# A hybrid decoder layer: VectorE, ScalarE and SyncE put into program order, with loads further ahead

## The chip, the cores and the metric

The kernel runs on one core of a Trainium2 chip. The metric is the device time of one execution in microseconds (us). TensorE (PE) does the matrix products, VectorE (DVE) and ScalarE (ACT) the elementwise work, GpSimd (POOL) a few powers, and SyncE (SP) issues nearly all DMAs. Each of these engines takes its instructions from one queue.

## The reference

One decoder layer over 256 tokens of 2048 features, in float32:

```python
hn = rmsnorm(h, norm_mix_w[l])
q, k, v, g_ret, xr, yr, g_a, g_b = jnp.split(hn @ w_in[l], offsets, axis=-1)
...
ret = head_groupnorm(chunkwise_retention(q, k, v), ret_gn_w[l]).reshape(b, s, D_RET_V)
ret_out = jax.nn.silu(g_ret) * ret
xr = causal_dwconv(xr, rnn_conv_w[l], rnn_conv_b[l])
hr = rg_lru(xr, rg_w_a[l], rg_b_a[l], rg_w_x[l], rg_b_x[l], rg_lambda[l])
rnn_out = jax.nn.gelu(yr) * hr
merged = (jax.nn.sigmoid(g_a) * (ret_out @ w_proj_ret[l])
          + jax.nn.sigmoid(g_b) * (rnn_out @ w_proj_rnn[l]))
h = h + merged @ w_mix_out[l]
...
h = h + memory_cross_attention(hn, mem_n, xa_w_q[l], xa_w_k[l], xa_w_v[l], xa_w_o[l])
...
h = h + conv_gated_ffn(hn, ffn_w_up[l], ffn_conv_w[l], ffn_conv_b[l], ffn_w_down[l])
return rmsnorm(h, final_norm_w)
```

Retention has 8 heads with rotary positions; the RG-LRU is a gated recurrence over the tokens (here four blocks of 512 features); the cross-attention has 4 heads over 256 memory tokens; the FFN is 5632 wide, with a convolution over three tokens ahead of its gate.

## The kernel before

All weights lie in one stream in the order of use (`weight_plan`). A chunk of it is four tiles of 128 rows by 512 columns, 1 MB, loaded by SP into one of three `raw` buffers. `prefetch` splits each chunk into a rounded part `hi` (ACT, two instructions) and the rest `lo` (DVE, two instructions), in six buffers each, which is three chunks; the products x_hi·w_hi + x_lo·w_hi + x_hi·w_lo on TensorE stand for a float32 product. One chunk is 24 matmuls of 512 columns, or as much in other shapes. Before the matmuls of chunk c are written down, the chunks up to c+2 are split (`AHEAD`), so the split of c+3 is written behind everything that follows chunk c. It needs the `hi` and `lo` buffers of chunk c.

Four chunks make a product of 256 tokens by 512 columns. Its result is read out of PSUM (`turned_rows`: DVE writes `rows`), cut by ACT into 16-bit planes (`by_dma`: `pl`, two copies), transposed by two DMAs (`pt`), and joined by ACT (`f`, two copies). The call `later(n, fn)` has a function run n + 1 chunks further on; the joins, the attention scores and the recurrence are written in this way between the chunks.

The parts that the change and the prediction touch, in the order of the layer:

- `tables` and `rotated`: sine and cosine, and the rotation of q and k (ta, tb, an add, and a split into s by ACT and DVE).
- `retain`: scores, values, and `normalise`, which scales the rows of each head (rc, on DVE) and writes them (ACT), two tiles of two pairs of heads each.
- `conv_x`, `recur`, `gelu_y`, once for each of the four blocks of the RG-LRU: the convolution over four tokens (one ACT and three DVE instructions for each of four tiles, `xr`); the gates with small products on TensorE, tanh and exp on ACT, a square root, and a scan on DVE; and the gelu of the other branch, the product `rn`, and its split into s. `RG_WAIT` sets how many chunks the recurrence comes behind the convolution.
- `gated`: the sigmoid gates of the merge; `residual`: adding to the residual rows, their squares and their transposes; `memory_steps`: the norm of the memory; `gate_up`: the gated product of the FFN and its split.

What sets the order: matmuls and the small transposes on TensorE are kept in the order of the program (`mm`, `turn_small`). All else is ordered by the tile scheduler, which places each instruction by its priority and by when it expects the operands; `high_priority` moves the evacuation and the planes ahead. So on ACT, DVE and SP a split may stand ahead of work that was written before it.

Of the kernel before, what the change touches and what calls it, by code (L numbers as in the profile page):

```python
# [36 lines left out]
FREE = 300  # L37
RG_WAIT = 3
EPS = 1e-6
# [88 lines left out]


@with_exitstack  # L130
def hybrid_layer(
# [72 lines left out]

    def mm(*a, **k):
        tc.keep_in_program_order(pe.matmul(*a, **k))  # L206

    def turn_small(*a):
        tc.keep_in_program_order(pe.transpose(*a))  # L209

# [15 lines left out]
    at = [0]  # L226

    def prefetch(n):
        while len(ahead) < n and taken[0] < len(stream):
            i = taken[0]  # L230
            name, row, nk, c = stream[i]
            taken[0] += 1
            size = nk * P * BW
            src = wall[at[0] : at[0] + size].rearrange("(p k n) -> p k n", p=P, k=nk)
            at[0] += size
            raw = wp.tile([P, KC, BW], F32, tag="raw", bufs=RAW_BUFS, name=nm("raw"))
            k2 = row // (KH * P)
# [3 lines left out]
            if own:  # L241
                xs.load(k2 + 1)
            for a, b in zip(cuts, cuts[1:]):
                sp.dma_start(out=raw[:, a:b, :], in_=src[:, a:b, :])  # L244
                if i == 0 and a == 0:
                    sp.dma_start(out=xs.rest[0], in_=xs.rest[1])
                elif own and a == 0:
                    xs.load(k2 + nk // KH)
# [10 lines left out]
            for k in range(0, nk, KH):  # L259
# [13 lines left out]
                parts.append((hi, lo))  # L273
            ahead.append(((row, c), parts))
            if i >= 4:
                load_x(min(4, i - 3))
# [30 lines left out]
    def steps_t(w, row, st, nk, col):  # L307
# [4 lines left out]
        for k0, n, parts in chunks(nk, w, row, col):  # L312
            last = k0 + n >= nk
            tiles = [(kk, j) for j in range(2) for kk in range(n)]
            if first and k0 == 0:
                runs = [[(t, pr, kk, j) for t in (0, 1)] for kk in range(n) for pr in range(2) for j in range(2)]
            elif last:
                runs = [[(t, pr, kk, j) for kk, j in tiles] for pr in range(2) for t in (1 - pr, pr)]
            else:
                runs = [[(t, pr, kk, j) for pr in range(2) for kk, j in tiles] for t in (phase, 1 - phase)]  # L320
                phase = 1 - phase
            for i, run in enumerate(runs):
                for t, pr, kk, j in run:
                    k = k0 + kk
                    sx = st[k // 2][:, k % 2, :]
                    part = parts[kk // KH][t][:, kk % KH, (2 * pr + j) * P : (2 * pr + j + 1) * P]
                    a = accs[pr][:, j, :]
                    if t == 1:
                        a, sx = a[:, S:BW], sx[:, 0:S]
                    mm(  # L330
                        a, part, sx, start=k == 0 and t == 0, stop=k == nk - 1 and t == 0, skip_group_check=True
                    )
# [7 lines left out]
    def products_n(o, sx, hi, lo, tt, start, stop):  # L340
        h = sx[:, tt * P : (tt + 1) * P]
        l = sx[:, S + tt * P : S + (tt + 1) * P]
        mm(o, h, hi, start=start, stop=False)
        mm(o, l, hi, start=False, stop=False)
        mm(o, h, lo, start=False, stop=stop)

# [16 lines left out]
    def product(o, l, r, start, stop):  # L363

        for i, (a, b) in enumerate(((l[0], r[0]), (l[0], r[1]), (l[1], r[0]))):
            mm(o, a, b, start=start and i == 0, stop=stop and i == 2, skip_group_check=True)

# [101 lines left out]
    def spread_tokens(r):  # L469
# [5 lines left out]
        def products():  # L475
            bc = small((P, S))
            for tt in range(2):
                cs = slice(tt * P, (tt + 1) * P)
                mm(bc[:, cs], ones, diag[:, cs], start=True, stop=True)
            act.copy(rsb, bc)  # L480
# [97 lines left out]
    qjoin = [joined(t, "q") for t in next(q_steps)]  # L578
    assert next(q_steps, None) is None
    later(0, tables)  # L580

# [21 lines left out]
    def retain(g, qr, kr, vs, dec, gates):  # L603
# [36 lines left out]
        def normalise():  # L640
            rows = [big([P, 2, BW], s="rows") for _ in range(2)]
            rstd = rsqrt_small(stats[:, :, 1], 8, 1.0, GN_EPS).rearrange("p (h t) -> p h t", t=2)
            for tt in range(2):
                dve.tensor_scalar_mul(rstd[:, :, tt], rstd[:, :, tt], rs0[:, tt : tt + 1])
            for hh in range(4):
                for tt in range(2):
# [5 lines left out]
                    )  # L652
                    act.mul(rows[hh // 2][:, tt, (hh % 2) * DV : (hh % 2 + 1) * DV], y, rstd[:, hh, tt : tt + 1])  # L653
            for i, r in enumerate(rows):
                by_dma(r, words.append, 2 + i)

# [64 lines left out]
    def recur(b, rgw, xr, pr, aa, tt_, ti):  # L721

        for j in (2 * pr, 2 * pr + 1):
# [3 lines left out]
            for i in range(2):  # L727
                mm(gp[:, i, :], rgw[:, i, j, :], xr[:, j, :], start=True, stop=True)
            tr = tp.tile([P, S], F32, tag="tr", bufs=2, name=nm("tr"))
# [17 lines left out]
        for j in range(4):  # L747
            dve.tensor_tensor_scan(
                out=xr[:, j, :], data0=aa[:, j, :], data1=ti[:, j, :], initial=0.0, op0=ALU.mult, op1=ALU.add
            )  # L750

    for b in range(4):
# [27 lines left out]
        def gelu_y(f, xr=xr):  # L780
            for pr in range(2):
                y = f[:, 2 * pr : 2 * pr + 2, :]
                y2, th = tmp("y2"), tmp("yt")
                act.activation(y2, y, AF.Square)
                dve.tensor_scalar(out=y2, in0=y2, scalar1=0.044715 * K0, scalar2=K0, op0=ALU.mult, op1=ALU.add)
                dve.tensor_tensor(out=y2, in0=y2, in1=y, op=ALU.mult)
                act.activation(th, y2, AF.Tanh)
                dve.scalar_tensor_tensor(out=y, in0=th, scalar=1.0, in1=y, op0=ALU.add, op1=ALU.mult)
            for pr in range(2):
                o = tmp("rn")  # L790
                cs = slice(2 * pr, 2 * pr + 2)
                dve.tensor_tensor(out=o, in0=xr[0][:, cs, :], in1=f[:, cs, :], op=ALU.mult)
                rnn.append(split_pair(o, 0.5))

        turned_rows(gemm_n("w_in", 0, xs, NT, O_XR + b * BW), rs0, conv_x)
        turned_rows(gemm_n("w_in", 0, xs, NT, O_YR + b * BW), rs0, gelu_y, 4 if b < 3 else 3)


# [29 lines left out]
    def residual(w, st, out, wcol, steps=None):  # L828

        ss = sums()  # L830
        for b in range(4):
            if steps:
                steps(b)
            h = hrow[b]
            dve.tensor_add(h, h, gemm_n(w, 0, st, NT, b * BW))  # L835
            squares(h, ss, b)
            by_dma(hrow[b], lambda f, b=b: turn(f, b, out, wcol))
        return ss
# [15 lines left out]
    def memory_steps(b):  # L854
        if b == 1:
            ss = sums()
            for c in range(4):
                sum_squares(mnat[c], ss, c)
            rsms.append(rstd_rows(ss))
        if b == 3:  # L860
# [35 lines left out]
    def transpose_probs(pr_):  # L896
        t = small()
        for kt in range(2):
            for tt in range(2):
                turn_small(t[:, kt, tt * P : (tt + 1) * P], pr_[:, tt, kt * P : (kt + 1) * P], ident)  # L900
        if done[0] == len(pTs):
# [68 lines left out]

    def gate_up(gt, vl, hid):
        for pr in range(2):
            cs = slice(2 * pr, 2 * pr + 2)
# [3 lines left out]
            dve.tensor_tensor(out=o, in0=o, in1=vl[:, cs, :], op=ALU.mult)  # L977
            hid.append(split_pair(o, 0.5))

# [120 lines left out]
```

## Time and profile before

| | us |
|---|---|
| median of 3 runs | 2023.56 |
| lowest and highest | 2022.26, 2023.94 |
| profiled execution | 2022.28 |
| its span, first to last instruction | 2020.5 |
| TensorE busy | 2002.3 |
| VectorE busy | 1264.3 |
| ScalarE busy | 1246.0 |

The span is shorter than the time by what lies around the program's first and last instruction. Busy time of TensorE counts matmuls whose ends are modelled, and they overlap, so it is not the time at its best rate; the distance of two matmuls' starts is. In rows of the timeline, the first number is the start in us from the start of the span, the second the duration; `x2` at the end says that two instructions are merged into the row, and the bracket gives the idle time of the engine before it and what ended it. In rows of groups, the numbers behind the bar are the total busy time, the mean in ns of one instruction, and the idle time before them. Line numbers are those of the kernel before; many instructions are issued by helpers, so a line can stand for many places (L206 for all matmuls, L269 and L270 for the splits).

### The profile page before, as it was taken

The page shows a single profiled execution, that of the slowest core. Times are in us where ns is not written, and L with a number is a line of the kernel's source. Part 1 is how long each engine was busy: PE and PEld are TensorE (multiplying, and loading weights), DVE is VectorE, ACT ScalarE, POOL GpSimd, SP SyncE. Part 2 cuts the span into 40 slices and gives each one's busy share as a digit, 9 for nine tenths or more (in the row PEclk, how much of TensorE's full clock was granted, in tenths as well). Part 3 has the DMA queues.
Part 4 walks back from the last instruction along what each step waited for, and adds up shares of the span by engine and source line. Part 5 has one row for each costly group of instructions (what it writes and reads, how often), then busy time and mean ns, then how long its engine had stood idle before and what let it go on. Part 6 is the DMA issues. An engine that isn't in the chain of part 4 may idle for free.

```text
span 2020.5 us, 23630 instructions
## 1 busy us (share of the span) xinstructions
PE 2002.3 (99%) x9060; PEld 1666.2 (82%) x9060; DVE 1264.3 (63%) x1563; ACT 1246.0 (62%) x1502; POOL 7.7 (0%) x12
## 2 busy tenths in 40 slices
PE   9999999999999999999999999999999999999998
PEld 7888888888888888788888888888888888888887
DVE  5856756888645555456555554567675577664675
ACT  6546547989434555478666556666774566644763
POOL 0000000000000000000000000000000000000000
PEclk9999999999999999999999999999999999999999
DMA  8665656665555566777766546667666566655663
GB/s 304 225 210 173 234 199 192 228 213 188 208 188 190 197 204 214 259 225 242 219 198 204 182 167 208 209 189 218 228 203 232 193 195 214 227 215 198 210 228 125
DMA packets 185153, 421.99 MB, mean 209 GB/s; under 512 B 127440, under 2 KB 132176, under 8 KB 139984
## 3 DMA queue, kind: packets, MB, share of 16 engines
q1 hardware_dynamic: 183520, 417.85, 62.2%
q10 hardware_dynamic: 1520, 2.63, 0.4%
q8 instruction: 71, 1.16, 0.2%
q14 instruction: 42, 0.34, 0.1%
HBM read 388.46 MB, written 2.10 MB: 193 GB/s over the span
## 4 chain that ended last, share of the span: by engine, by line
PE 97%; ACT 1%; DVE 1%; DMA 1%; issue 1%; SPq 0%; POOL 0%; POOLq 0%; DVEq 0%; ACTq 0%
PE acc L206 94%; PE sm L206 3%; DMA raw<-in_wall 1%; DVE lo L270 0%; ACT f L391 0%; DVE xr L765 0%; ACT pl L380 0%; ACT rows L653 0%; ACT hi L269 0%; POOL ro L507 0%; PE sm L209 0%; SPq L244 0%; DVE s L447 0%; ACT nat L1034 0%; DVE rows L404 0%
## 5 line engine op out<-in xcount | busy, mean ns | idle before, releaser
L206 PE MATMUL acc<-hi,s 128*128 128x512 f32 (+1 forms) x5680 | 1741.6, 388 | 4.2 <-ACT s L423 4.0
L270 DVE TENSOR_TENSOR lo<-raw,hi 128x1024 fp32r<-128x1024 f32 (+1 forms) x714 | 861.1, 1220 | 662.4 <-ACT hi L269 636.5
L206 PEld LDWEIGHTS acc<-hi,s 128*128 128x128 f32 x5680 | 1062.5, 188 | 222.1 <-ACT s L423 4.5
L206 PE MATMUL acc<-lo,s 128*128 128x512 f32 (+1 forms) x2840 | 1100.8, 388 | 2.0 <-DVE lo L270 2.0
L269 ACT CAST hi<-raw 128x1024 fp32r<-128x1024 f32 (+1 forms) x712 | 736.0, 1051 | 535.4 <-PE acc L206 466.7
L206 PEld LDWEIGHTS acc<-lo,s 128*128 128x128 f32 x2840 | 533.7, 188 | 111.6 <-DVE lo L270 2.7
L391 ACT COPY f<-pt 128x1024 uint16<-128x1024 uint16 x114 | 146.5, 1350 | 68.8 <-DMA pt<-pl 68.6
L380 ACT COPY pl<-rows 128x1024 uint16<-128x1024 uint16 x90 | 89.8, 1046 | 66.1 <-DVE rows L404 58.2
L404 DVE TENSOR_SCALAR rows<-acc,ro 128x512 f32<-128x512 f32 x68 | 47.8, 747 | 2.4 <-PE acc L206 2.4
L957 DVE SCALAR_TENSOR_TENSOR fv<-f,pf,fv 128x255 f32<-128x255 f32 (+1 forms) x88 | 35.8, 479 | 0.7 <-ACT fv L955 0.7
L957 DVE SCALAR_TENSOR_TENSOR fg<-f,pf,fg 128x255 f32<-128x255 f32 (+1 forms) x88 | 35.6, 478 | 0.0
L955 ACT ACTIVATE fv<-f,pf 128x256 f32<-128x256 f32 x44 | 22.9, 596 | 0.0
L955 ACT ACTIVATE fg<-f,pf 128x256 f32<-128x256 f32 x44 | 22.9, 594 | 0.0
L423 ACT ACTIVATE s<-fo 128x512 fp32r<-128x512 f32 x22 | 13.6, 635 | 14.1 <-DVE fo L977 14.1
L380 ACT COPY pl<-nat 128x1024 uint16<-128x1024 uint16 x16 | 16.0, 1046 | 9.6 <-DVE nat L835 9.6
L765 DVE SCALAR_TENSOR_TENSOR xr<-f,pa,xr 128x255 f32<-128x255 f32 (+2 forms) x48 | 20.1, 481 | 2.1 <-ACT xr L763 2.0
L446 ACT ACTIVATE s<-f,pb 128x256 fp32r<-128x256 f32 x48 | 20.4, 501 | 0.0
L447 DVE SCALAR_TENSOR_TENSOR s<-f,pb,s 128x256 fp32r<-128x256 f32 x48 | 19.9, 480 | 0.0
L206 PEld LDWEIGHTS sm<-s,s 128*128 128x128 f32 x144 | 18.8, 191 | 0.9
L206 PE MATMUL acc<-s,hi 128*128 128x512 f32 x64 | 17.6, 413 | 1.0 <-DVE hi L267 1.0
L206 PE MATMUL sm<-s,s 128*128 128x256 f32 (+1 forms) x144 | 18.6, 279 | 0.0
L421 DVE TENSOR_TENSOR s<-f,s 128x512 fp32r<-128x512 f32 x16 | 10.3, 687 | 10.0 <-ACT s L420 10.0
(154 smaller groups left out, 630.0 us busy)
## 6 DMA issues: line engine op xcount, KB each, us to landing
raw<-in_wall SPq DMA_DIRECT2D x352, 1024.0 KB, 4.9
raw<-in_wall SPq DMA_DIRECT2D x6, 512.0 KB, 6.4
nat<-in_x ACTq DMA_DIRECT2D x4, 512.0 KB, 8.2
nat<-in_x SPq DMA_DIRECT2D x4, 512.0 KB, 5.7
nat<-in_mem SPq DMA_DIRECT2D x4, 512.0 KB, 9.0
xt<-in_mem_t SPq DMA_DIRECT2D x8, 256.0 KB, 3.7
pt<-pl SPq DMA_TRANSPOSE x114, 4.9
xt<-in_x_t SPq DMA_DIRECT2D x7, 256.0 KB, 6.3
```

Source lines behind the costliest of these rows:

```text
L206: tc.keep_in_program_order(pe.matmul(*a, **k))
L269: act.copy(hi[:, ds], raw[:, cs, :])
L270: dve.tensor_tensor(out=lo[:, ds], in0=raw[:, cs, :], in1=hi[:, ds].bitcast(F32), op=ALU.subtract)
L380: act.copy(planes[:, :, h, :], words[:, h])
L391: act.copy(halves_[:, h], turned_[:, h])
L404: dve.tensor_scalar_mul(rows[:, tt, :], a[:, tt, :], r[:, tt : tt + 1])
L423: act.mul(t[:, :, 0:S], src, scale)
L446: act.activation(t[:, j, 0:S], src[:, j, :], AF.Identity, scale=wcol(j))
L447: dve.scalar_tensor_tensor(out=t[:, j, S:BW], in0=src[:, j, :], scalar=wcol(j), in1=t[:, j, 0:S].bitcast(F32), op0=ALU.mult, op1=ALU.subtract,
L765: dve.scalar_tensor_tensor(out=y[:, s:S], in0=z[:, 0 : S - s], scalar=p_cw(3 - s, t), in1=y[:, s:S], op0=ALU.mult, op1=ALU.add,)
L955: act.activation(y, z[:, j, :], AF.Identity, scale=pf[:, 2, t : t + 1], bias=pf[:, 3, t : t + 1])
L957: dve.scalar_tensor_tensor(out=y[:, s:S], in0=z[:, j, 0 : S - s], scalar=pf[:, 2 - s, t : t + 1], in1=y[:, s:S], op0=ALU.mult, op1=ALU.add,)
```

## The change

`InOrder` wraps an engine so that each instruction issued through it is kept in program order. TensorE is wrapped from the start in place of the two helpers, and ACT, DVE and SP from the point at which the first q product is done. `load` issues the load of a chunk as soon as the chunk that had its buffer is split, three chunks ahead of its own split, instead of in the call that splits it. Work moves between the chunks: `normalise` writes one pair of heads, and the next a chunk later, both joined four chunks on; `gelu_y` keeps the gelu and leaves the product with the recurrence's result and its split to the next chunk (`times_y`); `RG_WAIT` is 2 in place of 3, and the last block's `gelu_y` waits 2 in place of 3; `residual` cuts the planes before the squares; the squares of the memory rows are taken one tile a chunk; `gate_up` splits its product a chunk later.

```diff
-RG_WAIT = 3
+RG_WAIT = 2
...
+class InOrder:
+    def __init__(self, tc, engine):
+        self.tc, self.engine = tc, engine
+
+    def __getattr__(self, name):
+        f = getattr(self.engine, name)
+        return lambda *a, **k: self.tc.keep_in_program_order(f(*a, **k))
...
-    def mm(*a, **k):
-        tc.keep_in_program_order(pe.matmul(*a, **k))
-
-    def turn_small(*a):
-        tc.keep_in_program_order(pe.transpose(*a))
+    pe = InOrder(tc, pe)
...
+    raws = []
+
+    def load(n):
+        while len(raws) < min(n, len(stream)):
+            i = len(raws)
+            nk = stream[i][2]
+            size = nk * P * BW
+            src = wall[at[0] : at[0] + size].rearrange("(p k n) -> p k n", p=P, k=nk)
+            at[0] += size
+            raw = wp.tile([P, KC, BW], F32, tag="raw", bufs=RAW_BUFS, name=nm("raw"))
+            raws.append((raw, src))
+            if i >= 2 * len(EARLY):
+                sp.dma_start(out=raw[:, 0:nk, :], in_=src)
...
+            load(i + 1)
+            raw, src = raws[i]
...
-            for a, b in zip(cuts, cuts[1:]):
+            for a, b in zip(cuts, cuts[1:]) if early else ():
...
+            if i >= 2 * len(EARLY):
+                load(i + 1 + RAW_BUFS)
...
     assert next(q_steps, None) is None
+    act, dve, sp = (InOrder(tc, e) for e in (act, dve, sp))
     later(0, tables)
...
         def normalise():
-            rows = [big([P, 2, BW], s="rows") for _ in range(2)]
...
-                    act.mul(rows[hh // 2][:, tt, (hh % 2) * DV : (hh % 2 + 1) * DV], y, rstd[:, hh, tt : tt + 1])
-            for i, r in enumerate(rows):
-                by_dma(r, words.append, 2 + i)
+
+            def two_heads(i):
+                rows = big([P, 2, BW], s="rows")
+                for hh in (2 * i, 2 * i + 1):
+                    for tt in range(2):
+                        c = (hh % 2) * DV
+                        act.mul(rows[:, tt, c : c + DV], raws[hh][:, tt, :], rstd[:, hh, tt : tt + 1])
+                by_dma(rows, words.append, 4)
+
+            for i in range(2):
+                later(i, lambda i=i: two_heads(i))
...
+    def times_y(f, xr):
+        for pr in range(2):
+            o = tmp("rn")
+            cs = slice(2 * pr, 2 * pr + 2)
+            dve.tensor_tensor(out=o, in0=xr[:, cs, :], in1=f[:, cs, :], op=ALU.mult)
+            rnn.append(split_pair(o, 0.5))
...
         def gelu_y(f, xr=xr):
-            for pr in range(2):
-                y = f[:, 2 * pr : 2 * pr + 2, :]
-                y2, th = tmp("y2"), tmp("yt")
+            halves_ = [(f[:, 2 * pr : 2 * pr + 2, :], tmp("y2"), tmp("yt")) for pr in range(2)]
+            for y, y2, _ in halves_:
                 act.activation(y2, y, AF.Square)
                 dve.tensor_scalar(out=y2, in0=y2, scalar1=0.044715 * K0, scalar2=K0, op0=ALU.mult, op1=ALU.add)
                 dve.tensor_tensor(out=y2, in0=y2, in1=y, op=ALU.mult)
+            for y, y2, th in halves_:
                 act.activation(th, y2, AF.Tanh)
                 dve.scalar_tensor_tensor(out=y, in0=th, scalar=1.0, in1=y, op0=ALU.add, op1=ALU.mult)
-            for pr in range(2):
-                o = tmp("rn")
-                cs = slice(2 * pr, 2 * pr + 2)
-                dve.tensor_tensor(out=o, in0=xr[0][:, cs, :], in1=f[:, cs, :], op=ALU.mult)
-                rnn.append(split_pair(o, 0.5))
+            later(0, lambda: times_y(f, xr[0]))
...
-        turned_rows(gemm_n("w_in", 0, xs, NT, O_YR + b * BW), rs0, gelu_y, 4 if b < 3 else 3)
+        turned_rows(gemm_n("w_in", 0, xs, NT, O_YR + b * BW), rs0, gelu_y, 4 if b < 3 else 2)
...
             dve.tensor_add(h, h, gemm_n(w, 0, st, NT, b * BW))
+            by_dma(hrow[b], lambda f, b=b: turn(f, b, out, wcol))
             squares(h, ss, b)
-            by_dma(hrow[b], lambda f, b=b: turn(f, b, out, wcol))
...
             for c in range(4):
-                sum_squares(mnat[c], ss, c)
-            rsms.append(rstd_rows(ss))
+                later(c, lambda c=c: sum_squares(mnat[c], ss, c))
+            later(4, lambda: rsms.append(rstd_rows(ss)))
...
     def gate_up(gt, vl, hid):
+        rows = []
...
-            hid.append(split_pair(o, 0.5))
+            rows.append(o)
+        later(0, lambda: hid.extend(split_pair(o, 0.5) for o in rows))
```

More of the change, by code (lines that the diff above doesn't have):

```diff
@@ L232, in prefetch @@
             taken[0] += 1
[L233 to L236, printed above, removed]
+            load(i + 1)
+            raw, src = raws[i]
             k2 = row // (KH * P)
@@ L329, in steps_t @@
                         a, sx = a[:, S:BW], sx[:, 0:S]
-                    mm(
+                    pe.matmul(
                         a, part, sx, start=k == 0 and t == 0, stop=k == nk - 1 and t == 0, skip_group_check=True
@@ L342, in products_n @@
         l = sx[:, S + tt * P : S + (tt + 1) * P]
-        mm(o, h, hi, start=start, stop=False)
-        mm(o, l, hi, start=False, stop=False)
-        mm(o, h, lo, start=False, stop=stop)
+        pe.matmul(o, h, hi, start=start, stop=False)
+        pe.matmul(o, l, hi, start=False, stop=False)
+        pe.matmul(o, h, lo, start=False, stop=stop)
     def steps_n(w, row, st, nk, col):
@@ L365, in product @@
         for i, (a, b) in enumerate(((l[0], r[0]), (l[0], r[1]), (l[1], r[0]))):
-            mm(o, a, b, start=start and i == 0, stop=stop and i == 2, skip_group_check=True)
+            pe.matmul(o, a, b, start=start and i == 0, stop=stop and i == 2, skip_group_check=True)
     def halves(t, j, cs=slice(0, S)):
@@ L478, in products @@
                 cs = slice(tt * P, (tt + 1) * P)
-                mm(bc[:, cs], ones, diag[:, cs], start=True, stop=True)
+                pe.matmul(bc[:, cs], ones, diag[:, cs], start=True, stop=True)
             act.copy(rsb, bc)
@@ L727, in recur @@
             for i in range(2):
-                mm(gp[:, i, :], rgw[:, i, j, :], xr[:, j, :], start=True, stop=True)
+                pe.matmul(gp[:, i, :], rgw[:, i, j, :], xr[:, j, :], start=True, stop=True)
             tr = tp.tile([P, S], F32, tag="tr", bufs=2, name=nm("tr"))
@@ L899, in transpose_probs @@
             for tt in range(2):
-                turn_small(t[:, kt, tt * P : (tt + 1) * P], pr_[:, tt, kt * P : (kt + 1) * P], ident)
+                pe.transpose(t[:, kt, tt * P : (tt + 1) * P], pr_[:, tt, kt * P : (kt + 1) * P], ident)
         if done[0] == len(pTs):
```

## The prediction

> **What bounds the kernel now.** I read the page first, then who waits on TensorE, then the chain of waits.
>
> ```profile
> span 2020.5 us, 23630 instructions
> PE 2002.3 (99%) x9060; PEld 1666.2 (82%) x9060; DVE 1264.3 (63%) x1563; ACT 1246.0 (62%) x1502; POOL 7.7 (0%) x12
> PE 97%; ACT 1%; DVE 1%; DMA 1%; issue 1%; SPq 0%; POOL 0%; POOLq 0%; DVEq 0%; ACTq 0%
> ```
> ```profile
> PE acc L206 <- ACT s L423: 4.0, 1, 4.0
> PE acc L206 <- DVE lo L270: 3.9, 5, 2.0
> ```
> ```profile
> 340.31 3.92 PE acc L206 x16
> 353.14 38.09 PE acc L206 x168
> 846.35 84.08 PE acc L206 x359
> 1211.86 792.03 PE acc L206 x3528
> ```
> TensorE is the bound and stops only twice after the start: 2.0 us before 340.31 and 4.0 us before 846.35. Between them it runs without a hole (the last row: 3528 matmuls in 792 us). A chunk is 24 matmuls of 512 columns; 168 in 38.09 us is 5.44 us a chunk. Behind the second stop it also runs slower for a while:
>
> ```profile
> 846.35 1.52 PE L206 MATMUL acc<-hi,s 128*128 128x512 f32 x2 [4.04 <-ACT s L423]
> 848.10 1.05 PE L206 MATMUL acc<-hi,s 128*128 128x512 f32 x2
> 848.95 0.63 PE L206 MATMUL acc<-lo,s 128*128 128x512 f32 x1
> 851.57 0.63 PE L206 MATMUL acc<-hi,s 128*128 128x512 f32 x2
> ```
> From 848.10 to 848.95 two matmuls take 0.85 us, 0.427 each; by 851.57 a pair's row is 0.63 long instead of 1.05. Some 10 matmuls cost 0.2 us more, 2.0 us, and the first three 0.7 more than that. Behind the 2.0 us stop nothing of the kind shows. So the most that the change can win is 2.0 + 4.0 + 2.7 + about 0.3 of small waits = 9.0 us; start and tail keep their order of instructions but for a few.
>
> The other engines are 62% busy on average, but not everywhere:
>
> ```profile
> 361.00:385.00 24.00, 24.00 (x108) 19.87 (x107) 22.38 (x32) 23.58 (x29) 0.00 (x0) 1.00 0.59 194
> 408.00:455.00 47.00, 47.00 (x210) 39.07 (x209) 39.36 (x54) 41.68 (x55) 0.00 (x0) 1.00 0.71 213
> ```
> The third and fourth busy times are DVE and ACT. Where the RG-LRU blocks follow one another, ACT has 0.4 us to spare in 24, then 5.3 in 47. What the order there is worth is seen here:
>
> ```profile
> 420.36 1.06 ACT L269 CAST hi<-raw 128x1024 fp32r<-128x1024 f32 x1
> 421.72 1.06 ACT L269 CAST hi<-raw 128x1024 fp32r<-128x1024 f32 x1 [0.30 <-PE acc L206]
> 422.68 1.15 ACT L423 ACTIVATE s<-rn 128x512 fp32r<-128x512 f32 x2
> 423.74 2.56 ACT L391 COPY f<-pt 128x1024 uint16<-128x1024 uint16 x2
> 426.32 2.08 ACT L763 ACTIVATE xr<-f,pa 128x256 f32<-128x256 f32 x4
> 428.31 1.99 ACT L269 CAST hi<-raw 128x1024 fp32r<-128x1024 f32 x2
> ```
> ```profile
> 421.37 1.29 DVE L792 TENSOR_TENSOR rn<-xr,f 128x512 f32<-128x512 f32 x2
> 423.70 1.29 DVE L424 SCALAR_TENSOR_TENSOR s<-rn,s 128x512 fp32r<-128x512 f32 x2
> 426.96 1.40 DVE L765 SCALAR_TENSOR_TENSOR xr<-f,pa,xr 128x255 f32<-128x255 f32 x3 [0.83 <-ACT xr L763]
> 428.27 1.41 DVE L404 TENSOR_SCALAR rows<-acc,ro 128x512 f32<-128x512 f32 x2
> 429.59 3.23 DVE L765 SCALAR_TENSOR_TENSOR xr<-f,pa,xr 128x253 f32<-128x253 f32 x8
> ```
> The scheduler runs the gated product (rn, s) before the next block's convolution (f, xr) and lets the weight splits (hi) in between and right behind the four xr. ACT never waits for the convolution.
>
> **The change, part by part.** In program order a split for chunk c+3 stands behind everything that falls due after chunk c. It can wait two chunks, 10.9 us from the end of c, plus 0.45 us, since lo is read by the chunk's third matmul. Whatever chain stands ahead of it on ACT or DVE for longer stops TensorE.
>
> *Convolution ahead of the product (three times, blocks 1 to 3).* ACT's queue now reads f f, four xr, s, s, hi hi; DVE's reads 12 convolution steps, rn, s, rn, s, lo lo. From the start of f, with the rows above: f 2.56 and the first xr 0.5, DVE starts at 3.0; 12 steps at 0.40 take 4.9, to 7.9; rn 0.69, ACT s 0.62, DVE s 0.69, rn 0.69, ACT s 0.62: 11.3; hi 1.05 and lo 1.22: 13.6. ACT idles some 4 us of this with hi behind it. For no stop f has to begin 13.6 - 11.35 = 2.2 us before the end of c. It can't: the chunk before has this on ACT,
>
> ```profile
> L787 ACT ACT_TABLE_LOAD x4 | 5.1, 1283 | 0.1
> L787 ACT ACTIVATE yt<-y 128x512 f32<-128x512 f32 x8 | 5.1, 634 | 2.0 <-DVE y L786 1.9
> L784 ACT ACTIVATE y<-f 128x512 f32<-128x512 f32 x8 | 5.0, 627 | 0.0
> L380 ACT COPY pl<-rows 128x1024 uint16<-128x1024 uint16 x90 | 89.8, 1046 | 66.1 <-DVE rows L404 58.2
> L748 DVE TENSOR_TENSOR_SCAN xr<-aa,ti 128x256 f32<-128x256 f32 x16 | 9.7, 672 | 0.0
> ```
> f 2.56, two y 1.2, a table 1.28, two yt 1.2, hi hi 2.0, with overlaps 8.0; ahead of it rows on DVE 1.4, pl pl 2.0 and hi hi 2.0, 5.4 from a chunk end two chunks earlier. So f begins no sooner than 5.4 + 8.0 - 10.9 = 2.5 us after the end of c, and the stop is 2.5 + 2.2 = 4.7 at the least. DVE comes about 1.7 late to the rows, because the scans (4 x 0.6) and two lo of the recurrence stand ahead: 6.3. At the first of the three the joins of two pairs of heads (2 x 2.5) are still queued, and the recurrence starts late: 7.5. Sum 20.1. Each stop is over 4 us, so each brings the slow matmuls, 2.0: 6.0 more (0 and 2.7 at the ends).
>
> [...]
>
> *Rotation and first heads.* The rotation's price:
>
> ```profile
> 54.18 0.28 DVE L563 CAST rot<-posi 128x256 f32<-128x256 int32 x1
> 57.14 1.22 DVE L270 TENSOR_TENSOR lo<-raw,hi 128x1024 fp32r<-128x1024 f32 x1
> 60.34 0.42 DVE L576 TENSOR_TENSOR cos<-cos,rsb 128x256 f32<-128x256 f32 x1
> 60.79 0.69 DVE L588 TENSOR_TENSOR ta<-q,cos 128x512 f32<-128x512 f32 x1
> 61.50 1.38 DVE L590 TENSOR_TENSOR tb<-q,sin 64x512 f32<-64x512 f32 x2
> 63.52 0.69 DVE L594 TENSOR_TENSOR ta<-ta,tb 128x512 f32<-128x512 f32 x1
> 181.36 0.36 DVE L644 TENSOR_SCALAR ro<-ro,ro 128x4 f32<-128x4 f32 x2 [1.54 <-POOL ro L507]
> ```
> One pair: ta 0.7, tb 1.4, add 0.7, ACT's s 0.65, DVE's s 0.65, 4.1. Tables start at 51.0 in the new order (3.0 to the last rot, 1.7 for sin and cos), then hi, lo, lo (to 58.5), two pairs (ACT's second s at 66.0), v (0.7 and 0.6 on ACT), hi, lo: lo at 69.4, where TensorE wants it at 66.75: 2.7 us. The same rotation returns at 190, behind `normalise`. There the eight rc products, all of which now stand behind the root (last row: DVE has ro at 181.4 to 182.0), hold DVE at 0.40 each until 185.3 and lo, lo until 187.5, just in time for the chunk at 187.7. ACT has four rows until 184.2, pl pl until 186.2, hi hi until 188.1, f f until 190.6; the rotation's add ends at 193.5, ACT's s at 194.1, the second four rows at 195.8, pl pl at 197.7, hi at 198.65, lo at 199.9, where TensorE wants it at 199.05: 0.9 us. Behind it stand the second pair (ACT's s ends at 204.4), v v and hi, so that lo comes at 207.9 where it is wanted at 205.35: 2.5. Together 3.4. Bounds of the two places: 0, if the scheduler's places for hi cost nothing to lose, and 10, if a slow phase follows each.
>
> *Second group into the first convolution (315 to 375).* Two heads a time relieve 326 to 334, but a recurrence one chunk earlier finds ACT busy: its third gate product waits 0.8 for a PSUM buffer, the scans put lo 1.1 late, `gelu_y` the next 0.4; at the last block's product, 1.2. 3.5 (0 to 8).
>
> *What is removed.* 2.0 before 340: that order is gone. 4.0 + 2.7 at 846: the join of the last merged block now stands two splits earlier in ACT's queue, m, m 2.4, pl 2.0, landing, f 2.5, s 1.3 after the end of its chunk, about 15.5 of the 16.3 us there are. 0.3 of small waits. -9.0.
>
> *At no cost.* Loads:
>
> ```profile
> raw<-in_wall SPq DMA_DIRECT2D x352, 1024.0 KB, 4.9
> DMA to landing us min/median/max: 3.1/4.9/7.3
> ```
> A load lands in 4.9 (first row) of the 16.3 us that three buffers give; TensorE never waits for one, so issuing it earlier wins nothing, and SP's in-order wait for a lo holds only transposes whose rows stand behind that lo anyway (if it held one, 4.9 once). The split of `gate_up` a chunk later, planes ahead of squares, memory sums over four chunks: covered by chunks that have two splits and nothing else (without that cover 2.4 a block, 0, and 6.4 once). The eight loads of x and mem stay behind the last transposes on SP; the recurrence's weights are loaded before it as they were.
>
> **Sum.** 20.1 + 6.0 + 2.7 + 3.4 + 3.5 - 9.0 = +26.7. The profiled execution took 2022.28 (0.06% under the median of 2023.56): **2049 us**.
>
> **Rivals.** *The order costs nothing and both stops go*: 2022.3 - 9.0 = 2013. For it: averages of 62 and 63%, and two chunks of slack. Against: ACT's 0.4 in 24 us. It decides if f of the convolution begins 2.2 us before the chunk end, that is, 4.7 earlier than I find. 8%; in between, no measurable change 4%. *Only the least stops*: 3 x 4.7, no slow matmuls, nothing else: +14.1 - 9.0, 2027; 14%. *The FFN joins it*: a gate and a value take 8 chunks, 43.5 us, and DVE's chain through them (rows, pl, landing, f, convolution, product, lo, twice) is about 41.5 with landings of 4.5 us and 44.8 with 6.2; the second row above has 4.9 and up to 7.3 from one issue, and there are two. Then 1.3 for each of 11 blocks: 2063; 16%. For it, in 1319 to 1363, the waits of f for pt; against, a load issued before the rows has landed when the planes are ready. The forecast keeps 58% (2036 to 2060).
>
> The range goes from 2025 to 2068. What a measurement can tell from no change is about 0.2%, 4 us: faster 0.08, same 0.04, slower 0.88.
>
> **What would show it.** Right: waits of TensorE for hi and lo near 66, 200 and 380 and twice more 55 us apart, each of these three over 4 us; ACT waiting for DVE's rn in front of s; no wait at 846. Wrong: hi cast ahead of s at those places, TensorE stopping in the FFN, or a whole trace without stops.

## The result, and the profile after

The changed kernel takes 2075.15 us (median), the kernel before 2023.44 in the same runs: a ratio of 1.0255, 95% interval 1.0238 to 1.0273, 52 us slower. Forecast were 2049 and a range of 2025 to 2068: the sign was right and the size too small by half. In the profiled executions the spans are 2020.5 and 2070.7, +50.2.

The page of the changed kernel (span; busy time; shares of the chain that ended last):

```profile
span 2070.7 us, 23537 instructions
PE 2017.9 (97%) x9060; PEld 1670.4 (81%) x9060; DVE 1279.2 (62%) x1563; ACT 1234.5 (60%) x1502; POOL 8.3 (0%) x12
PE 81%; ACT 7%; DVE 6%; DMA 3%; issue 2%; SPq 0%; POOL 0%; POOLq 0%; ACTq 0%; DVEq 0%
```

DVE and ACT have about the work that they had (1279.2 and 1234.5 us for 1264.3 and 1246.0), and yet they now hold 13% of the chain, where they had 2%. Who makes TensorE wait (us in total, times, longest), and two pieces of the chain (start, length, what):

```profile
PE acc L138 <- ACT hi L138: 32.2, 10, 7.6
PE acc L138 <- DVE lo L138: 4.5, 8, 1.0
PE sm L138 <- DVE ps L138: 3.2, 4, 1.1
PE sm L138 <- ACT ps L138: 1.4, 1, 1.4
```
```profile
552.56 330.36 PE acc L138 x1456
1257.64 772.52 PE acc L138 x3408
```

The two stops of before are gone, and ten waits for hi have come. The second fence shows where nothing happens: 772 us of the FFN run without a hole.

The difference between the starts of the same matmul in the two profiles, taken every 24 matmuls, steps up at these places:

| place (us, profile after) | forecast | measured |
|---|---|---|
| start, up to the first heads | 0 | -2.2 |
| rotation, 68 | 2.7 | 6.7 |
| first normalise and rotation, 203 and 212 | 3.4 | 6.0 |
| three convolution stops, 398, 454, 511 | 20.1 | 22.4 |
| what follows those stops | 6.0 | 7.7 |
| second group, first block (343, 553) | 3.5 | 3.2 |
| stops removed | -9.0 | -9.1 |
| mixed output and memory, 890 to 985 | 0 | 4.8 |
| cross-attention, 1140 to 1256 | 0 | 5.9 |
| last columns of the FFN, 2045 | 0 | 4.1 |
| the rest | 0 | 0.7 |
| sum | 26.7 | 50.2 |

The first of the long stops in the trace (start, length, engine, operation; in brackets the idle time before it and what ended it):

```profile
384.36 2.57 ACT L138 COPY f<-pt 128x1024 uint16<-128x1024 uint16 x2
386.96 2.08 ACT L138 ACTIVATE xr<-f,pa 128x256 f32<-128x256 f32 x4
387.60 5.82 DVE L138 SCALAR_TENSOR_TENSOR xr<-f,pa,xr 128x255 f32<-128x255 f32 x12 [1.70 <-ACT xr L138]
393.33 0.68 DVE L138 TENSOR_TENSOR rn<-xr,f 128x512 f32<-128x512 f32 x1
394.05 0.63 ACT L138 ACTIVATE s<-rn 128x512 fp32r<-128x512 f32 x1 [5.00 <-DVE rn L138]
396.04 0.63 ACT L138 ACTIVATE s<-rn 128x512 fp32r<-128x512 f32 x1 [1.36 <-DVE rn L138]
397.63 1.22 DVE L138 TENSOR_TENSOR lo<-raw,hi 128x1024 fp32r<-128x1024 f32 x1 [0.24 <-ACT hi L138]
397.65 1.22 PE L138 MATMUL acc<-hi,s 128*128 128x512 f32 x2 [7.56 <-ACT hi L138]
```

This is the chain of the forecast, link by link: f, four xr, twelve steps, rn and s twice, hi. From the start of f to TensorE's first matmul it takes 13.3 us, to the end of lo 14.5 (forecast 13.6). ACT stands still for 5.0 us with hi behind the s that waits.

### The profile page after: what moved, and what is told of

Same layout as the page of the kernel before. It is cut to its first block, busy times and chain, and to the rows that moved or that the text cites. A ratio compares the mean times of both kernels' runs of the same rounds, so it can differ in the third digit from the quotient of the medians.

```text
span 2070.7 us, 23537 instructions
## 1 busy us (share of the span) xinstructions
PE 2017.9 (97%) x9060; PEld 1670.4 (81%) x9060; DVE 1279.2 (62%) x1563; ACT 1234.5 (60%) x1502; POOL 8.3 (0%) x12
## 4 chain that ended last, share of the span: by engine, by line
PE 81%; ACT 7%; DVE 6%; DMA 3%; issue 2%; SPq 0%; POOL 0%; POOLq 0%; ACTq 0%; DVEq 0%
PE acc L138 79%; PE sm L138 2%; DVE lo L138 2%; ACT hi L138 2%; DMA raw<-in_wall 2%; ACT f L138 1%; DVE xr L138 1%; DMA nat<-in_x 1%; ACT s L138 0%; ACT pl L138 0%; DMA xt<-in_mem_t 0%; DMA posi<-in_positions 0%; ACT junk L138 0%; ACT tt L138 0%; ACT L138 0%
## 5 line engine op out<-in xcount | busy, mean ns | idle before, releaser
L138 DVE TENSOR_TENSOR lo<-raw,hi 128x1024 fp32r<-128x1024 f32 x694 | 819.0, 1221 | 402.5 <-ACT hi L138 389.6
L138 ACT CAST hi<-raw 128x1024 fp32r<-128x1024 f32 x694 | 695.6, 1048 | 272.7 <-PE acc L138 251.6
L138 DVE SCALAR_TENSOR_TENSOR fg<-f,pf,fg 128x255 f32<-128x255 f32 x88 | 39.6, 481 | 33.8 <-ACT fg L138 32.2
L138 DVE SCALAR_TENSOR_TENSOR fv<-f,pf,fv 128x255 f32<-128x255 f32 x88 | 39.6, 481 | 28.3 <-ACT fv L138 26.7
L138 DVE TENSOR_TENSOR nat<-nat,acc 128x1024 f32<-128x1024 f32 (+1 forms) x23 | 24.8, 1080 | 46.4 <-PE acc L138 46.4
L290 DVE TENSOR_TENSOR lo<-raw,hi 128x1024 fp32r<-128x1024 f32 (+1 forms) x20 | 21.9, 1117 | 11.0 <-ACT hi L289 10.8
L138 ACT ACTIVATE sig<-acc,half_rs 128x512 f32<-128x512 f32 x16 | 10.1, 685 | 30.2 <-PE acc L138 30.2
L138 DVE SCALAR_TENSOR_TENSOR s<-f,pb,s 128x256 fp32r<-128x256 f32 x48 | 20.1, 482 | 11.6 <-ACT s L138 11.6
L138 ACT ACTIVATE junk<-nat 128x512 f32<-128x512 f32 x30 | 18.6, 622 | 11.1 <-DVE nat L138 11.1
L138 ACT ACTIVATE v<-acc,ro 128x512 fp32r<-128x512 f32 x16 | 11.0, 687 | 22.0 <-PE acc L138 13.8
```

Of the source, the lines that this page charges most:

```text
L138: return lambda *a, **k: self.tc.keep_in_program_order(f(*a, **k))
L290: dve.tensor_tensor(out=lo[:, ds], in0=raw[:, cs, :], in1=hi[:, ds].bitcast(F32), op=ALU.subtract)
```

## Experiments

**Which part of the change.** First the order without the rest, the rest without the order, and the order on some engines only.

```
 # kernel before, behind q_steps
+    act, dve, sp = (InOrder(tc, e) for e in (act, dve, sp))
```

> The kernel before, with nothing changed but that VectorE, ScalarE and SyncE keep the program's order from the first heads on. Theory (the fixed order of ScalarE and VectorE makes the stops, because splits of weights stand behind everything that falls due): slower than before by 20 to 60 us, 2043 to 2083, with stops of TensorE for hi and lo in the recurrent blocks and no slow loads. Rival (the loads three chunks ahead and the regrouping cost the time, the order does not): 2018 to 2029, as before.

2513.6 us, a ratio of 1.242 (1.240 to 1.244): 491 us slower, outside both expectations. Why shows in who makes ScalarE wait:

```profile
ACT hi L138 <- DMA raw<-in_wall: 516.0, 110, 19.6
```

A load is written right ahead of its split. My reading, tested below with the loads put back: in the order of the program it is issued behind the transposes written before it, and these wait for their planes.

```
 # changed kernel
-    act, dve, sp = (InOrder(tc, e) for e in (act, dve, sp))
```

> The changed kernel without the fixed order on VectorE, ScalarE and SyncE: loads three chunks ahead and all the regrouping stay, the scheduler orders the rest. Theory (order): 2012 to 2030, no stop over 4 us near 390, 447 and 503. Rival (loads and regrouping): 2045 or more, with most of the stops of the changed kernel still there.

2025.9, 1.0014 (1.0005 to 1.0023): 3 us slower. The stop of before at 340 is gone, the one at 846 stays, and two waits for lo of 1.8 and 2.0 us come in the first recurrent block. So neither half alone gives the result; 49 of the 52 us (2025.9 to 2075.2) come with the order, on a kernel that the other half has made fit for it.

```
-    act, dve, sp = (InOrder(tc, e) for e in (act, dve, sp))
+    sp = InOrder(tc, sp)
```

> The changed kernel with the order fixed on SyncE alone. Theory (ScalarE and VectorE): within 6 us of the same kernel with no order fixed. Rival (transposes and loads queued behind one another on SyncE delay f by 2 us or more per block): at least 15 us slower than that kernel.

2032.6: 6.7 more than with no order fixed, just over the bound of the theory. The recurrent blocks lose some 4 us each, and the stop at 846 goes.

```
-    act, dve, sp = (InOrder(tc, e) for e in (act, dve, sp))
+    act, dve = (InOrder(tc, e) for e in (act, dve))
```

> The changed kernel with the order fixed on ScalarE and VectorE, and SyncE left to the scheduler. Theory: 2065 to 2080, the three stops of 7.2 to 7.6 us stay within 1 us. Rival (SyncE): 2050 or less, the stops at most 5 us.

2072.1, a ratio of 1.0244: as the theory has it; SyncE's order makes no difference that these runs resolve.

```
 # changed kernel, in prefetch
-            if i >= 2 * len(EARLY):
-                load(i + 1 + RAW_BUFS)
```

> The changed kernel, but each load of weights is issued where the kernel before issues it, right ahead of its split, instead of three chunks ahead. Theory (with SyncE in program order a load stands behind transposes that wait for their planes, so that the 490 us of the order alone are the loads): 2350 to 2520, ScalarE's hi waiting for raw in most chunks. Rival (the regrouping is what makes the order bearable, the loads are hidden anyway): 2070 to 2100.

2481.1, 1.226 (1.224 to 1.229), as the theory has it, with

```profile
ACT hi L138 <- DMA raw<-in_wall: 526.8, 108, 19.6
```

So in the fixed order the early loads are worth 406 us and the regrouping about 32 (2513.6 to 2481.1).

**One engine.**

```
-    act, dve, sp = (InOrder(tc, e) for e in (act, dve, sp))
+    act = InOrder(tc, act)       # or: dve = InOrder(tc, dve)
```

> The changed kernel with the order fixed on ScalarE alone, VectorE and SyncE left to the scheduler. Theory (the stops come from ScalarE and VectorE waiting for one another in turn: s on ScalarE behind twelve convolution steps on VectorE): 2035 to 2055, each of the three stops 5.5 us at most. Rival (ScalarE's order alone makes them): 2062 or more, the stops as long as with both fixed.

> The changed kernel with the order fixed on VectorE alone. Theory (waiting in turn): 2030 to 2055, stops shorter than 6 us and now for lo, since hi may pass. Rival (VectorE's order alone makes them): 2062 or more. If ScalarE alone makes them: 2030 or less.

2052.7 and 2070.7. Who makes TensorE wait, with ScalarE's order fixed and then with VectorE's:

```profile
PE acc L138 <- DVE lo L290: 16.1, 9, 4.6
```
```profile
PE acc L138 <- DVE lo L138: 33.1, 12, 7.7
```

ScalarE's order alone came out as the theory has it (the three stops are 4.0 to 4.6 us, for lo). VectorE's order alone costs nearly all: hi passes now, but lo stands where it stood. That is the rival, not my theory of two engines that must both be fixed.

**The three stops.** The product ahead of the convolution, where both fall due:

```
-            for _, fn in due:
-                fn()
+            first = [p for p in due if len(p) > 2]
+            for p in first + [p for p in due if len(p) == 2]:
+                p[1]()
...
-            later(0, lambda: times_y(f, xr[0]))
+            pending.append((step[0] + 1, lambda: times_y(f, xr[0]), 1))
```

> The changed kernel with its fixed order, but where the gated product and the convolution fall due after the same chunk, the product comes first in the program. Theory (s behind twelve convolution steps holds hi, 5 of the 13.2 us from f to the split): hi no longer waits for VectorE's convolution, lo still stands behind it; the three stops become 3 to 6 us for lo, 2055 to 2068. Rival (the sum of the work ahead of the split sets the stop, in whatever order): stops of 7 us or more, 2070 to 2080.

2076.0: the rival. Each stop is now 4.2 to 4.6 for hi and 3.4 for lo, as long as before in sum. The convolution a chunk later, the recurrence where it was:

```
-RG_WAIT = 2
+RG_WAIT = 1
-        turned_rows(gemm_n("w_in", 0, xs, NT, O_XR + b * BW), rs0, conv_x)
+        turned_rows(gemm_n("w_in", 0, xs, NT, O_XR + b * BW), rs0, conv_x, 2)
```

> The changed kernel with its fixed order, but the convolution falls due one chunk later than the gated product, the recurrence staying where it is. Theory (the sum of the work that one split stands behind sets the stop; product and convolution in one chunk are too much): each of the three stops falls to 4.5 us or less, 2050 to 2066. Rival (ScalarE and VectorE are late by then whatever the chunk, the stop moves along): stops of 7 us or more a chunk later, 2071 or more.

2072.5: the time is the rival's. The stops fell as the theory has it, none is over 2.3 us, but several small waits in each block add up to as much. Less work instead of another place:

```
-                for s in range(1, 4):
+                for s in range(4, 4):
```

> The changed kernel without the twelve steps of VectorE in each block's convolution (only the first tap is computed, so the recurrent branch is another function). Theory (the chain from f to the split, 13.2 us, sets the stop, and 5.8 of it are these steps; a stop under 2.5 us is followed by no slow matmuls): the three stops fall from 7.2 to 7.6 to 1 to 2.5 us and lose the 2 to 3.3 us of slow matmuls, 2046 to 2056. Rival (the stop is set by f's landing and ScalarE's own work): stops of 5 us or more, 2066 or more.

2057.7, 17.5 us less. The stops are 2.1 to 2.4, as forecast; the slow matmuls stay (a mean granted clock of 0.97 from 444.80 to 496.61, fourth fence below), against the forecast.

The last of the three fits the forecast's chain; the first two don't fit a stop that the lateness of one chunk sets. All three agree with another reading. In the stretch from one stop to the next (length; busy PE, PEld, DVE, ACT; clock), the kernel before (nearly the same stretch of one block, 210 matmuls), the changed one, the one with the convolution later, and the one without the twelve steps:

```profile
427.00:474.00 47.00, 47.00 (x210) 39.07 (x209) 39.36 (x54) 40.92 (x54) 0.00 (x0) 1.00 0.65 213
```
```profile
397.65:453.87 56.22, 48.98 (x208) 39.84 (x208) 40.35 (x54) 40.28 (x54) 0.00 (x0) 0.92 0.60 178
```
```profile
458.68:514.40 55.72, 50.51 (x208) 39.59 (x209) 40.34 (x54) 40.16 (x53) 0.00 (x0) 0.97 0.56 179
```
```profile
444.80:496.61 51.81, 49.19 (x208) 40.05 (x208) 34.81 (x42) 40.21 (x54) 0.00 (x0) 0.97 0.59 193
```

A block is 47 us of matmuls. VectorE's and ScalarE's 40 fit into that only if they wait for no more than some 7 us. What VectorE waits for, before and after, in these stretches:

```profile
DVE ti L740 <- ACT ti L731: 2.7, 2, 1.4
DVE xr L765 <- ACT xr L763: 1.7, 2, 0.8
DVE rows L404 <- PE acc L206: 1.6, 1, 1.6
DVE lo L270 <- ACT hi L269: 1.4, 1, 1.4
```
```profile
DVE lo L138 <- ACT hi L138: 6.7, 5, 3.0
DVE a L138 <- ACT aa L138: 3.0, 2, 1.5
DVE y L138 <- ACT y L138: 1.7, 1, 1.7
DVE xr L138 <- ACT xr L138: 1.7, 1, 1.7
DVE s L138 <- ACT s L138: 1.4, 2, 0.7
```

After, with 1.0 of smaller ones, 15.5 us, all for ScalarE and none for TensorE; 40.35 + 15.5 is 55.9 of the 56.2. (ScalarE waits 15.5 for VectorE in return: 9.1 for rows, 6.4 for rn.) The sum alone shows nothing, since busy and idle time always add up to the stretch; what it shows is for whom VectorE waits. ScalarE waits for TensorE by 0.4 us only, for the gate products of the block (tr for sm); up to these, 15.5 us from the end of the stop, the chain that ended last runs over TensorE, and from there to the next stop over ScalarE and VectorE. The reading: the pair paces the block, each engine waiting for the other in turn, and TensorE only shows the difference to its own 47. Shifting work would leave that sum, and 5.5 us less of VectorE's work makes the stretch 4.4 to 5.3 shorter. The reading was tested by taking one wait away, the 6.7 of lo, at the price of later transposes:

```
 # turned_rows, in the recurrent blocks only
+        prefetch(AHEAD + 1)
         by_dma(rows, then, wait)
```

> The changed kernel with its fixed order, but in the recurrent blocks each split is written between the rows and their two planes instead of behind the planes. New theory (a recurrent block lasts as long as VectorE's work, 40.3 us, plus its waits for ScalarE in the fixed order, 15.9 in 56.2 us, of which 6.7 are lo behind hi behind the planes; TensorE only shows the difference): about 5 us less a block, 51 us, 2056 to 2064. Rival (the first theory: the lateness of f at one chunk sets each stop, and the transposes now start 2 us later): stops as long or longer, 2074 to 2084.

2069.0, 6 us faster than the changed kernel, outside both expectations: 2.6 to 2.9 less in two of the three blocks, 0.5 in the first, half of what the new reading said, and the other way than the first. Its stretch and its waits:

```profile
451.47:506.01 54.54, 49.16 (x208) 39.91 (x208) 40.15 (x54) 40.65 (x54) 0.00 (x0) 0.94 0.58 183
```
```profile
DVE a L138 <- ACT aa L138: 6.2, 2, 3.4
DVE y L138 <- ACT y L138: 2.9, 1, 2.9
DVE lo L138 <- ACT hi L138: 0.7, 3, 0.2
ACT tr L138 <- PE sm L138: 2.4, 2, 1.8
```

The wait for hi fell by 6.0 as meant; those for aa and y rose by 4.4. ScalarE comes late there, and in part because of TensorE: its wait for the gate products rose from 0.4 to 2.4 us (last row). So the pair alone doesn't pace the block once it is a little faster, and the reading is borne out by half.

**The slow matmuls.**

```
 # conv_x, blocks 1 to 3, due where the stop is
+            def idle_work():
+                o = small().rearrange("p a s -> p (a s)")
+                for _ in range(28):
+                    pe.matmul(o, xs[0][:, 0, 0:P], xs[1][:, 0, :], start=True, stop=True)
+
+            if b:
+                later(1, idle_work)
```

> The changed kernel with 28 matmuls of no use (6.4 us at 0.228) put on TensorE at the place of each of the three long stops, their result read by nobody. Theory (the 2.0 to 3.3 us of slow matmuls behind a stop come from TensorE's idleness, not from what the other engines do at that time): the slow matmuls of the three places go, 2064 to 2069, while hi and lo come no earlier. Rival (they come from the burst of casts, hi and lo back to back, beside the matmuls): 2073 to 2078, unchanged.

2074.0 (2072.4 to 2074.3), not told apart from 2075.2. The stops shrink to 0.8 to 1.2 us. Behind the first and the third the slow matmuls are gone, which in the profile wins some 3 us; behind the second they stay, and at 551 new ones come, 1.6. So the run speaks for idleness as their cause, but not for the length of one gap: gaps of 1.2 and 0.5 us are followed by a granted clock of 1.00 at the first stop (401.5 to 405.0) and of 0.51 at the second (457.5 to 461.0; more on this at the end). What they cost didn't come back in the time.

**Where the order is lifted.** `fixed` sets the order of ScalarE, VectorE and SyncE on or off.

```
+    fixed(False)                       # ahead of the recurrent blocks
     for b in range(4):
         rgw = big([P, 2, 4, P], s="rgw")
...
+    fixed(True)                        # ahead of mb
```

> The changed kernel with the fixed order lifted in the four recurrent blocks alone (from the first convolution chunk to the gates of the merge). Theory (30 us of the loss, three stops with their slow matmuls, and some 3 us of small waits come from the order there): 2040 to 2050, no stop over 2.5 us between 350 and 560. Rival (the queues are late already when the blocks begin, the stops move to the place where the order is fixed again): 2060 or more.

2050.4, 25 us less, just over the theory's range: the 30 go, and the two waits for lo of the free order (1.8 and 2.0) come. The same lift kept from the end of the merge on, the blocks fixed:

```
+    fixed(False)
     hrow = [load_rows(x, c) for c in range(4)]
```

> The changed kernel with the fixed order lifted from the end of the merge on (mixed output, cross-attention, FFN). Theory (the 15 us of small waits behind 890, near 900, 975, 1175 to 1255 and 2045, come from the order): 2057 to 2064. Rival (they come from the memory sums spread over more chunks, the planes ahead of the squares and the later split of the gates): 2070 or more.

2066.0, 9 us less. The small waits behind 890 are gone (14.8), two of 1.0 and 0.5 come in the FFN, and the stop at 846, whose cure is the fixed order too, is back with 6.7, which I had left out of the expectation. So those 14.8 us don't come from the regrouping, which is still there, but with the order. For 2.7 of them, near 902, this run can't tell the order from the stop that came back at 846 (see the loads below).

**A version that beats both.** ScalarE's order fixed only from the last merged block to one chunk behind its join.

```
+        act.on = b == 3
         m = gated(O_GA, "w_proj_ret", ret, b, big([P, 2, BW], s="m"))
...
+        if len(merged) == 8:
+            later(0, lambda: setattr(act, 'on', False))
```

> No engine's order fixed but ScalarE's, and that only around the last merged block, where its join must stand ahead of the split behind it; loads and regrouping as changed, the recurrence three chunks behind as before. Theory (the two stops of before, 2.4 us at 340 and 6.7 us with its slow matmuls at 846, go and nothing comes): 2011 to 2018. Rival (the scheduler's own order finds another place to stop): 2020 to 2027.

This one, with the early loads and the regrouping and the two waits (RG_WAIT and the last `gelu_y`) back at 3, took 2033.8, more than both expectations: the stops at 340 and 846 went, but the recurrent blocks lost 16 us. With the waits at 2 and no order fixed they had lost some 4.5, so the rest comes with the longer waits; why isn't shown. The same on the kernel before, alone and with the gated rows two heads at a time:

> The kernel before with ScalarE's order fixed around the last merged block alone. Theory (the 4.0 us stop at 846 and its 2.7 us of slow matmuls come from a split that the scheduler put ahead of the join): 2014.5 to 2018. Rival (another wait takes its place there or behind): 2020 or more.

> The same with the gated rows of two heads at a time, as the changed kernel has them. Theory (the 2.4 us at 340 go too): 2012 to 2016. Rival (the regrouping of the heads moves the stop into the first convolution, as with the order left free, some 4 us): 2016 to 2021.

2020.9, 0.9992 (0.9983 to 1.0001), no difference, as the first rival has it; and 2017.9, 0.9977 (0.9968 to 0.9986), 5 us faster than before, the best here, in the range of the second rival:

```profile
span 2016.1 us, 23630 instructions
PE 2002.3 (99%) x9060; PEld 1666.8 (83%) x9060; DVE 1263.6 (63%) x1563; ACT 1242.0 (62%) x1502; POOL 7.7 (0%) x12
```

9.0 us go at 340 and 846, and 5.8 come back in small waits and slow matmuls from 860 to 933 (2.0 at 862, 3.6 at 925). With the memory sums spread over four chunks as well:

> The kernel before with ScalarE's order fixed around the last merged block, the gated rows two heads at a time, and the memory sums spread over four chunks. Theory (the 5.8 us of small waits that came up between 860 and 933 when the 6.7 at 846 went are ScalarE's and VectorE's burst of memory sums): 2012 to 2016. Rival (they are the late loads of the memory behind other loads): 2017 to 2020, as without the spread.

2020.2, 0.9987 (0.9978 to 0.9996): the 2.0 us at 862 go, as the theory has it, those at 925 grow to 5.4, and some more come in the FFN (1.2 at 1510). Who makes TensorE wait from 840 to 935, and who ScalarE:

```profile
PE acc L219 <- ACT s L459: 2.5, 1, 2.5
ACT s L459 <- DMA xt<-in_mem_t: 5.9, 2, 4.3
```

At 925 TensorE waits for the split of the memory rows, and ScalarE had waited 4.3 us for their load at 903.6; the chain that ended last runs over this load. That speaks for the rival at 925. That the load alone makes the stop isn't shown.

## Why the prediction was right or wrong

*Bound, removed stops, FFN.* Right. TensorE stops for hi and lo at the places named; -9.0 was forecast and -9.1 measured; the FFN stayed whole but for its last columns.

*Convolution ahead of the product.* The size was near (26.1, measured 30.1), and the chain stands in the trace: f begins 5.4, 4.9 and 4.9 us after the end of its chunk (forecast 5.3, 4.1, 4.1), and the twelve steps take 5.8 for 4.9. What didn't hold is that the stop is a matter of that one chunk, 2.2 + 2.5 + 1.7. With the product first or the convolution a chunk later the time stayed at 2072 to 2076 us, and VectorE's order alone does nearly all. My reading is that a block's mutual waits add up and come out at whatever place the slack ends; the run with the earlier split bore it out by half, so it is argued and not shown. What follows the stops was 1.9, 2.7 and 3.1 for 2.0 each, and filling the gaps won nothing that the runs resolve: this term should probably not have been added to the stops in full.

*Rotation and first heads.* The first chain ended where it was forecast (lo at 69.2 for 69.4), but TensorE came 2.2 us sooner than in the profile of before, and slow matmuls followed at both places (a granted clock of 0.50 from 66.46 to 73.28 and from 213.23 to 216.65). 6.1 forecast, 12.7 measured, over the upper bound of 10: the second term that was too small.

*Second group.* 3.5 forecast and 3.2 measured, but as 1.3 at 343 and 2.0 at 551, where 2.3 and 1.2 were forecast in the first convolution and at the last block's product: the sum is near in part by luck.

*At no cost: the step that failed.* The sum put everything behind the merge at nothing ("covered by chunks that have two splits and nothing else", and a tail that keeps its order "but for a few"). It measured 14.8 us, of the 23.5 that the sum lacks; with the order lifted there, these waits are gone (for 2.7 of it, near 902, see the loads). I had looked for cover where the change edits the program, and not where the order alone moves a split. At the end of the FFN, for example, before and after:

```profile
1990.53 1.22 DVE L998 TENSOR_TENSOR nat<-nat,acc 128x1024 f32<-128x1024 f32 x1
1991.78 0.64 ACT L850 ACTIVATE junk<-nat 128x512 f32<-128x512 f32 x1 [1.04 <-DVE nat L998]
1993.74 1.05 ACT L269 CAST hi<-raw 128x1024 fp32r<-128x1024 f32 x1 [0.62 <-ACT junk L850]
```

```profile
2041.87 1.22 DVE L138 TENSOR_TENSOR nat<-nat,acc 128x1024 f32<-128x1024 f32 x1
2043.12 0.63 ACT L138 ACTIVATE junk<-nat 128x512 f32<-128x512 f32 x1 [2.60 <-DVE nat L138]
2043.75 0.61 ACT L138 ACTIVATE junk<-nat 128x512 f32<-128x512 f32 x1
2044.36 1.97 ACT L138 CAST hi<-raw 128x1024 fp32r<-128x1024 f32 x2
2045.44 0.50 PE L138 MATMUL acc<-hi,s 128*128 128x256 f32 x2 [1.54 <-ACT hi L138]
```

The scheduler had put nat between VectorE's two lo (1989.39 and 1991.66); in program order it comes behind both. So each last chunk has a sum of squares that waits for VectorE, with hi behind it: 5.84 us a chunk (2032.68, 2038.53 and 2044.36 are the hi of three in a row), where TensorE takes 5.44 and in the last columns less. In the cross-attention ps stands behind two hi (the waits of TensorE for ps in the second profile fence of the result), where before it stood ahead of them.

*Loads.* That issuing them earlier wins nothing agrees with the run without the order (loads and regrouping, 3 us slower); alone they were not run on the kernel before. In the fixed order they are worth 406 us; "at no cost" was right for the change as a whole and said nothing of why it was made so. One load does reach TensorE, near 902. Three loads of weights are issued behind the eight loads of x and of the memory (SPq rows: start, length of the row), and land 13.6 to 14.9 us later, where the forecast took 4.9; ScalarE waits for them, and the chain that ended last runs from such a load over ScalarE's sums to the stop:

```profile
877.35 2.29 SPq L138 DMA_DIRECT2D nat<-in_mem  x4
879.74 17.47 SPq L138 DMA_DIRECT2D raw<-in_wall  x4
893.40 2.00 ACT L138 CAST hi<-raw 128x1024 fp32r<-128x1024 f32 x2 [10.74 <-DMA raw<-in_wall]
884.14 14.10 DMA raw<-in_wall
```

In the kernel before, the same loads take 12.1 to 13.5 us, but TensorE stands still ahead of 846 at that time. In the last two versions, where that stop is gone and SyncE's order is free, ScalarE waits for such a load as well (10.5 and 10.3 us, at 848); in the first of them the chain runs from it to the stop at 862, and with the memory sums spread that stop goes.

## What to carry to other kernels

Where two engines work for a third in a fixed order, look at one stage's work of each engine and at its waits for the other beside the stage's length on the third; here, where a stop showed said little about what made it. Count every place at which an order changes, not only those that the edit touches. A part of a change that is worth nothing alone (early loads and regrouping, 3 us slower) can be what another part needs: measure both alone.

## What the runs showed of the chip

In this case the clock also halved without one long gap. In the run with the gaps filled, the profile has these stretches at the second place (PEclk is the number behind POOL):

```profile
454.00:455.40 1.40, 0.27 (x2) 0.00 (x0) 0.69 (x1) 1.40 (x3) 0.00 (x0) 1.00 0.00 0
455.40:457.50 2.10, 1.49 (x5) 0.97 (x6) 2.04 (x2) 2.10 (x4) 0.00 (x0) 1.00 0.00 0
457.50:461.00 3.50, 3.50 (x10) 2.68 (x9) 3.50 (x5) 0.77 (x1) 0.00 (x0) 0.51 0.61 176
```

TensorE was idle for 1.2 us and 0.5 us within 3.5, and in the next 3.5 its granted clock was 0.51. Two gaps of 1.2 and 0.5 us near 902 in the changed kernel were followed by nothing of the kind:

```profile
899.31:902.72 3.41, 2.23 (x10) 1.42 (x8) 0.51 (x1) 3.41 (x7) 0.00 (x0) 1.00 0.90 270
902.72:906.13 3.41, 2.88 (x13) 2.17 (x12) 2.65 (x3) 3.41 (x7) 0.00 (x0) 1.00 0.55 90
```

In the changed kernel's profile the records of the granted clock have half clock from 66.46, 213.23, 394.14, 448.75, 506.78 and 2046.19 us, for 3.41 to 10.24 us each (and again from 2066.67, behind TensorE's last matmul), and the distances are 43, 53, 16, 17 and 451 times 3.413 us: these six lie on one grid. Near 902 a border of it, at 902.72, lies between the two gaps; that this spared the clock there is my reading, and no run here tests it. In the 3.41 us ahead of the six places TensorE was busy for 1.20, 1.02, 0.00, 1.34, 0.43 and 1.62 us, and in the 3.41 us up to 902.72, with full clock behind, for 2.23. In the kernel before it was 1.44 in the 3.41 us ahead of 844.28, from where the granted clock was 0.50 for 6.83 us.
